# A two-block transformer on one core: the state space scan as a pipeline of eight blocks, its tables made earlier, and the experts' row tables made two experts ahead

## The chip, the cores and the metric

The kernel is one program on one core of a Trainium2 chip. The metric is the device time of one execution in microseconds (us), lower being better. The core has five engines with a queue each, and each queue runs in order: PE (matrix products), DVE (VectorE, elementwise), ACT (ScalarE, elementwise with functions), POOL (GpSimd, slow elementwise and indirect DMA), SP (SyncE, which here only issues DMAs). They meet at semaphores. [...] A planner places the instructions into the queues when the program is built: it walks through them by a priority, which is the order of the program with offsets, and by a simulated time line.

## The reference, cut to what matters

All of it is float32, batch 1, 512 tokens of width 1024. A first block (a retention and pooling mixer, 32 experts of which each token takes 4, a gated embedding layer called PLE) is followed by a second block with a state space layer, a feed-forward layer, a short convolution and another feed-forward layer. The two places that matter are these:

```python
# experts: gather the tokens of each expert, two products, scatter-add with the gate
flat_e = top_idx.reshape(-1); order = jnp.argsort(flat_e); tok = order // TOP_K
gu = lax.ragged_dot(xt[tok], w_gu, group_sizes) + b_gu[sorted_e]
...
# state space: 64 groups, 64 complex states each, 16 channels per group
abr = mag * jnp.cos(li * dt);  abi = mag * jnp.sin(li * dt)
...
_, _, xr, xi = lax.associative_scan(_ssm_combine, (a_r, a_i, bu_re, bu_im), axis=1)
y = einsum('ghp,blgp->blgh', c_re, xr) - einsum('ghp,blgp->blgh', c_im, xi) + d * h
y = jax.nn.gelu(y);  val, gate = jnp.split(y @ w_out, 2, -1);  return val * jax.nn.sigmoid(gate)
```

## The kernel before, in words

Large products are made in three passes each (high part by high part, high by low, low by high); `split` makes the two parts of a weight block with one ACT copy (L94) and one DVE subtraction (L95).

**Mixer** (`stage_mix`, about 0 to 245 us). Beside its own work it prepares the state space layer in the background: `S5Prepare.units` makes powers 0 to 8 of the complex state factor (`s_ar`, `s_ai`) and, on POOL and DVE, sixteen products `s_pp` (`power_product`, L1117 to L1121), which PE transposes. Background units are given out by `net.step`, with a priority 400 places later than where they stand. The mixer ends with the output product `w_out`, made in two halves. During the second half `Router` makes the norm of the hidden rows (`hnm`, POOL, L648), the logits, and the place of each token in its expert.

**Experts** (`Moe.experts`, about 286 to 1490 us). For expert e, `tables` turns the places into a table of the 88 rows to fetch (`tabim`: eight or more DVE comparisons L719, small PE products, DVE L725 to L727); one call makes it for two or four experts. `fetch` issues the indirect gather of these rows into `xg` (L744, POOL; two buffers), `prepare` transposes them on PE (`xt`, L758) and splits them. In the loop over e, `tables(e+1)` and `fetch(e+1)` stand at the head of turn e, `prepare(e+1)` behind `down(e-1)` in the middle of it. Weight blocks (`raw`, 1 MB) are loaded through nine buffers.

**State space layer** (`stage_s5`, about 1557 to 1771 us). The 512 tokens are 64 chunks of 8. For each of eight blocks k of 128 channels: `norm` (DVE, ACT), `to_chunks` (`zt`: 8 PE transposes, two copies), `to_groups` (`zu`: 8 transposes, a copy), `states` (`zs`: 32 products that give each chunk's own input to the state, a copy to `zX`). Then `scan` goes over the 63 chunk steps one by one, in two halves (blocks 0 to 4 and 5 to 7): a DVE product (L1518) and a DVE reduction (L1520) for each step and half. Then come `within` and `outputs` (`zy`, 16 products each, with the tables T and Q), `to_features` (`zf`, 32 products, GELU, split into `zgah` and `zgal`) and the product `ssm_out`. The table Q is made here: `readout` computes it on POOL (three operations of 128x512 for each of 16 parts) and sends it by SP to `q_d`, from where `load_q` takes it back.

## Time and profile before

| | us |
|---|---|
| three runs | 2694.55, 2701.68, 2705.07 |
| median | 2701.68 |
| profiled execution, its own time | 2704.24 |
| its span, first to last instruction | 2701.8 |
| PE busy in the span | 2558.8 (95%) |
| DVE busy | 1898.3 (70%) |
| ACT busy | 1374.8 (51%) |
| POOL busy | 430.1 (16%) |
| mean granted PE clock | 0.970 |

[...] "Busy" of an engine counts the time in which one of its instructions runs, waits inside an instruction included. PE's ends are modelled, so that consecutive products overlap a little in the list. The profiled execution's own time is 2.4 us more than its span, and 2.56 us more than the median.

### The profile page before, as it was taken

What the parts mean: (1) busy time and instruction counts of PE and PEld (TensorE: products, weight loads), DVE (VectorE), ACT (ScalarE), POOL (GpSimd) and SP (SyncE); (2) the same over time, 40 slices, a digit from 0 to 9 for tenths busy, and PEclk for the clock granted to TensorE, in tenths of its full rate; (3) what the DMA queues carried; (4) which work ended last, traced back from release to release, by engine and by line L of the source; (5) the groups of instructions that cost most, each with busy time, mean ns of one, the idle gap of its engine ahead of it and who ended that gap; (6) DMA issues with size and microseconds to landing.
All of it is one profiled execution on the core that took longest, in us unless ns stands there. A gap on an engine that the chain in (4) does not pass through costs nothing.

```text
span 2701.8 us, 31654 instructions
## 1 busy us (share of the span) xinstructions
PE 2558.8 (95%) x12270; PEld 1927.6 (71%) x12271; DVE 1898.3 (70%) x2410; ACT 1374.8 (51%) x1513; POOL 430.1 (16%) x252
## 2 busy tenths in 40 slices
PE   8999788999999999999999865999999999999998
PEld 6767555666666666666666755888788888888886
DVE  8974877999999999898988577775553544532333
ACT  7344565777777777777776644242122322322221
POOL 3362312031312112031200071000000000000000
PEclk9999898999999999999999987999999999999999
DMA  6435788999999999999996642754552222223221
GB/s 210 172 110 214 292 289 305 355 341 383 346 383 356 373 360 375 352 358 373 368 372 239 248 150 80 278 188 177 210 214 104 103 97 103 83 86 103 101 85 63
DMA packets 110432, 634.76 MB, mean 235 GB/s; under 512 B 16043, under 2 KB 21419, under 8 KB 43331
## 3 DMA queue, kind: packets, MB, share of 16 engines
q1 hardware_dynamic: 97971, 599.69, 59.6%
q0 software_dynamic: 11584, 28.27, 4.2%
q10 hardware_dynamic: 720, 4.72, 0.4%
q8 instruction: 98, 1.61, 0.2%
q14 instruction: 59, 0.48, 0.1%
HBM read 607.15 MB, written 28.61 MB: 235 GB/s over the span
## 4 chain that ended last, share of the span: by engine, by line
PE 66%; issue 18%; DMA 7%; DVE 6%; POOL 2%; ACT 2%; SPq 0%; POOLq 0%; DVEq 0%; ACTq 0%
PE gu L115 8%; PE gu L116 8%; PE gu L117 8%; PE mm L115 7%; PE mm L116 7%; PE mm L117 7%; PE dn L116 4%; PE dn L117 4%; PE dn L115 4%; DMA xg<-hn_d,tabim 2%; DMA acc_d<-y,tabim 2%; DMA raw<-in_w_ada 1%; PE mm L146 1%; DVE wl L95 1%; PE mm L147 1%
## 5 line engine op out<-in xcount | busy, mean ns | idle before, releaser
L95 DVE TENSOR_TENSOR el<-raw,eh 128x2048 fp32r<-128x2048 f32 (+1 forms) x396 | 874.5, 2221 | 99.3 <-ACT eh L94 93.2
L94 ACT ACTIVATE eh<-raw 128x2048 fp32r<-128x2048 f32 (+1 forms) x396 | 735.2, 1866 | 294.0 <-PE gu L117 209.9
L94 ACT ACTIVATE wh<-raw 128x1024 fp32r<-128x1024 f32 (+1 forms) x238 | 222.0, 981 | 478.2 <-PE mm L116 291.9
L116 PE MATMUL gu<-el,xh 128*88 128x512 f32 x1024 | 404.2, 395 | 0.0
L117 PE MATMUL gu<-eh,xl 128*88 128x512 f32 x1024 | 402.4, 393 | 0.0
L115 PE MATMUL gu<-eh,xh 128*88 128x512 f32 x1024 | 400.6, 397 | 0.0
L95 DVE TENSOR_TENSOR wl<-raw,wh 128x1024 fp32r<-128x1024 f32 (+1 forms) x238 | 265.5, 1148 | 79.9 <-ACT wh L94 79.6
L116 PE MATMUL mm<-nl,wh 128*128 128x512 f32 x816 | 318.3, 390 | 0.0
L115 PE MATMUL mm<-nh,wh 128*128 128x512 f32 x816 | 317.9, 390 | 0.0
L117 PE MATMUL mm<-nh,wl 128*128 128x512 f32 x816 | 316.8, 389 | 0.0
L117 PEld LDWEIGHTS gu<-eh,xl 128*88 128x88 f32 x1024 | 158.4, 155 | 78.4 <-issue 0.5
L116 PEld LDWEIGHTS gu<-el,xh 128*88 128x88 f32 x1024 | 158.9, 155 | 75.8 <-issue 0.5
L115 PEld LDWEIGHTS gu<-eh,xh 128*88 128x88 f32 x1024 | 158.3, 155 | 75.3 <-issue 0.3
L115 PE MATMUL dn<-eh,ath 128*88 128x512 f32 x512 | 204.0, 401 | 0.4
L116 PE MATMUL dn<-el,ath 128*88 128x512 f32 x512 | 202.5, 399 | 0.0
L117 PE MATMUL dn<-eh,atl 128*88 128x512 f32 x512 | 202.4, 396 | 0.0
L750 POOL DMA_INDIRECT acc_d<-y,tabim x32 | 93.8, 2931 | 633.0 <-ACT y L958 566.1
L744 POOL DMA_INDIRECT xg<-hn_d,tabim x32 | 142.2, 4444 | 318.9 <-PE xt L758 157.4
L115 PEld LDWEIGHTS mm<-nh,wh 128*128 128x128 f32 x816 | 153.2, 188 | 32.7
L117 PEld LDWEIGHTS mm<-nh,wl 128*128 128x128 f32 x816 | 153.2, 188 | 32.3
L116 PEld LDWEIGHTS mm<-nl,wh 128*128 128x128 f32 x816 | 153.2, 188 | 31.5
L1681 DVE TENSOR_TENSOR fs<-fs,mm 128x512 f32<-128x512 f32 x44 | 30.2, 687 | 205.8 <-PE mm L117 196.4
(468 smaller groups left out, 3925.7 us busy)
## 6 DMA issues: line engine op xcount, KB each, us to landing
raw<-in_w_gu SPq DMA_DIRECT2D x256, 1024.0 KB, 8.7
raw<-in_w_down SPq DMA_DIRECT2D x128, 1024.0 KB, 7.5
raw<-in_w_ada SPq DMA_DIRECT2D x45, 1024.0 KB, 4.9
raw<-in_w_ffn_in SPq DMA_DIRECT2D x44, 1024.0 KB, 4.8
raw<-in_w_ffn_out SPq DMA_DIRECT2D x32, 704.0 KB, 4.1
raw<-in_conv_in SPq DMA_DIRECT2D x12, 1024.0 KB, 4.9
raw<-in_ssm_out SPq DMA_DIRECT2D x8, 1024.0 KB, 5.0
raw<-in_w_out SPq DMA_DIRECT2D x4, 1024.0 KB, 4.8
```

The source lines that it names most:

```text
L94: nc.scalar.activation(h, x, AF.Copy)
L95: nc.vector.tensor_tensor(l, x, h.bitcast(F32), ALU.subtract)
L115: mm(ps, sh, mh, start=start, stop=False)
L116: mm(ps, sh, ml, start=False, stop=False)
L117: return mm(ps, sl, mh, start=False, stop=stop).ins
L146: self.nc.tensor.matmul(ps[c], wh, ah, start=k == 0, stop=False)
L147: self.nc.tensor.matmul(ps[c], wl, ah, start=False, stop=False)
L744: return net.nc.gpsimd.indirect_dma_start(out=dst, out_offset=None, in_=net.hn_d[:, :], in_offset=bass.IndirectOffsetOnAxis(ap=idx, axis=0 ...
L750: net.nc.gpsimd.indirect_dma_start(out=net.acc_d[:, :], out_offset=bass.IndirectOffsetOnAxis(ap=idx, axis=0), in_=src, in_offset=None, com ...
L1681: nc.vector.tensor_tensor(t, t, ps, ALU.mult)
```

## The change

Three things are changed, and some sizes with them.

The experts' row tables: turn e now makes `tables(e+2)`, in turn 0 too, while `fetch(e+1)` stays where it was. The number of weight blocks asked for ahead of the experts falls from 6 to 5 and from 9 to 8.

The scan: the state of a chunk step is turned back by its angle, so that its factor becomes real and `tensor_tensor_scan` runs over all chunks in one instruction. Each block k becomes a stage of a pipeline of its own: products with a cosine and sine table, an addition on POOL, the scan, products that turn it forward again, and four additions. The eight blocks run through `norm`, `to_chunks`, `to_groups`, `states`, `scan`, `outputs`, `to_features` with lags of 0 to 5.

The tables: `readout` moves to the end of the mixer, ahead of its output product, 11 of its 16 parts on POOL and 5 on DVE, and the cosine and sine tables are made beside it on DVE (`roots`, `turns`) and stored to `r_d`. The store to `e_d` and its loads go.

```diff
@@ stage_mix
         s5.rows(99)
+        net.bg = s5.tables(p2)
+        net.step(99)
@@ stage_mix_out
-        moe.prefetch(6)
+        moe.prefetch(5)
...
-        moe.prefetch(9)
+        moe.prefetch(8)
@@ Moe.experts
-            if e + 1 < NE:
-                if e:
-                    self.tables(e + 1)
-                    self.fetch(e + 1)
+            if e + 2 < NE:
+                self.tables(e + 2)
+            if e and e + 1 < NE:
+                self.fetch(e + 1)
@@ S5Prepare.tables (new)
+        u = pool.tile([128, 1280], F32, tag="w5", name="s_qu")
+        w = pool.tile([128, 1280], F32, tag="w5", name="s_turns")
...
+        def times(o, x, y, t):
+            for r, op in ((0, ALU.subtract), (1, ALU.add)):
+                vec.tensor_tensor(o[r], x[0], y[r], ALU.mult)
+                vec.tensor_tensor(t, x[1], y[1 - r], ALU.mult)
+                vec.tensor_tensor(o[r], o[r], t, op)
...
+        def roots():
...
+            for z in (lo, hi):
+                for n in (1, 2, 4):
+                    k = min(n, 7 - n)
+                    times(span(z, n + 1, n + k + 1), span(z, 1, k + 1), ...
+                if z is lo:
+                    times(span(hi, 1, 2), span(lo, 4, 5), span(lo, 4, 5), scratch[:, :H].unsqueeze(2))
+        def turns(b):
+            cs = self.pt.tile([128, 512], F32, tag="sb", name=f"s_tu{b}")
...
+            times([ov[:, r] for r in range(2)], ...
+            nc.sync.dma_start(net.r_d[:, b * 512:(b + 1) * 512], cs)
+        def readout(q, on_vector):
...
+            power_product(vec if on_vector else nc.gpsimd, t, ...
+            (nc.sync if on_vector else nc.gpsimd).dma_start(net.q_d[:, q * 512:(q + 1) * 512], t)
+        roots()
+        for q in range(G // GP):
+            readout(q, q % 3 == 2)
+            if q % 2:
+                turns(q // 2)
+            yield True
@@ stage_s5
+        def scan(k):
+            pv = sts.pop(k)
+            sh = [128, 4, 2, NCH]
...
+            nc.scalar.copy(ro[:, :, :, 1:], net.turn[:, 0, o]...to_broadcast([128, 4, 2, NCH - 1]))
+            def turned(x, sign):
+                w = [p2.tile(sh, F32, tag=f"zw{j}", ...) for j in range(2)]
+                tt(w[0], x, cos.unsqueeze(2).to_broadcast(sh), ALU.mult)
+                for r in range(2):
+                    if (r == 0) == (sign > 0):
+                        tt(w[1][:, :, r], x[:, :, 1 - r], sin, ALU.mult)
+                    else:
+                        nc.vector.scalar_tensor_tensor(w[1][:, :, r], x[:, :, 1 - r], -1.0, sin, ALU.mult, ALU.mult)
+                return w
+            w = turned(pv, 1)
+            nc.gpsimd.tensor_tensor(w[0], w[0], w[1], ALU.add)
+            x = p2.tile(sh, F32, tag="zx", name=f"zx{k}", bufs=2)
+            nc.vector.tensor_tensor_scan(x..., ro..., w[0]..., 0.0, ALU.mult, ALU.add)
+            w = turned(x, -1)
+            xq = XQ[k] = p2.tile([128, 2, 4, NCH], F32, tag="zxq", name=f"zxq{k}")
...
+            for h in range(2):
+                for r in range(2):
+                    i = slice(64 * h, 64 * h + 64)
+                    (nc.gpsimd if h == r else nc.vector).tensor_tensor(
+                        xq[64 * r:64 * r + 64, h, :, 1:], w[0][i, :, r, :NCH - 1], w[1][i, :, r, :NCH - 1], ALU.add)
...
+        for j in range(2):
+            nc.sync.dma_start(tv[:, 2048 * j:2048 * j + 2048], net.r_d[:, 2048 * j:2048 * j + 2048])
         load_t(0)
+        load_q(0)
         load_t(2)
-        with tc.high_priority(offset=-1000), tc.issue_after(net.rooted):
-            readout(net)
...
+        for n in range(NK + 6):
...
+            stage(norm, 0)
+            stage(to_chunks, 0)
+            stage(to_groups, 1)
+            stage(states, 2)
+            stage(scan, 2)
+            stage(outputs, 4)
+            if n in (5, 7):
+                load_q(n - 1)
+            stage(to_features, 5)
...
-        with tc.issue_after(net.scanned), tc.issue_after(net.kept):
-            net.linear_fm(a["ssm_out"], NK, lambda k: (gah[:, k], gal[:, k]), evac, rate=2)
+        net.linear_fm(a["ssm_out"], NK, lambda k: ga[k], evac, rate=2)
```

In `stage_s5` the copies of `to_chunks` all go to ACT, the high part of `to_features` to ACT and its low part to POOL, and the Q tables for blocks 0 to 3 sit in the two buffers `wh` of the weight splits, as the T tables of blocks 4 to 7 sit in `wl` before and after.

## Rows read from the trace of the kernel before

**Rows 1.** Page, busy time, share of the span and instructions.
```profile
PE 2558.8 (95%) x12270; PEld 1927.6 (71%) x12271; DVE 1898.3 (70%) x2410; ACT 1374.8 (51%) x1513; POOL 430.1 (16%) x252
```

**Rows 2.** Stretches of the state space layer: length, busy (count) by engine, clock, DMA.
```profile
1576.00:1600.00 24.00, 21.77 (x398) 20.14 (x398) 13.92 (x32) 20.05 (x34) 19.77 (x19) 1.00 0.35 123
1600.00:1650.00 50.00, 3.18 (x46) 2.96 (x44) 49.83 (x201) 16.36 (x42) 27.53 (x24) 0.56 0.26 95
1650.00:1678.00 28.00, 28.00 (x387) 26.87 (x387) 12.21 (x30) 17.55 (x31) 5.66 (x5) 0.93 0.37 130
```

**Rows 3.** Groups by line, DVE, 1560 to 1690 us: busy, mean ns, idle before.
```profile
L1518 DVE TENSOR_TENSOR zr<-a,zX 128x80 f32<-128x80 f32 (+1 forms) x124 | 47.7, 416 | 9.1 <-ACT zX L1497 8.3
L1520 DVE TENSOR_REDUCE zX<-zr 128x40 f32<-128x120 f32 (+1 forms) x124 | 26.5, 247 | 1.5 <-ACT zr L1516 0.5
```

**Rows 4.** PE in order of time: start, length, operation, count merged.
```profile
1574.40 1.20 PE L1493 MATMUL zs<-zU,s_pt 128*64 128x64 f32 x32
...
1578.32 1.09 PE L1472 MATMUL zt<-consts,zh 128*64 128x128 f32 x8
1579.34 0.71 PE L1480 MATMUL zu<-consts,zct 64*128 64x64 f32 x8
...
1594.44 8.46 PE L1562 MATMUL zy<-zT,zU 128*64 128x128 f32 x128
...
1662.48 2.65 PE L1573 MATMUL zy<-zQ,zxq 128*64 128x128 f32 x28
1665.06 1.90 PE L1583 MATMUL zf<-consts,zyt 64*64 64x64 f32 x32
...
1678.07 0.48 PE L146 MATMUL mm<-zgah,wh 128*128 128x512 f32 x1
```

**Rows 5.** DVE groups by form, 1560 to 1690 us, columns as in rows 3.
```profile
L1592 DVE TENSOR_TENSOR zgal<-zg,zgah 128x512 fp32r<-128x512 f32 x4 | 2.7, 683 | 0.0
```

**Rows 6.** DVE in order of time, two steps of the scan.
```profile
1586.36 0.24 DVE L1518 TENSOR_TENSOR zr<-a,zX 128x80 f32<-128x80 f32 x1
...
1591.13 1.02 DVE L1518 TENSOR_TENSOR zr<-a,zX 128x80 f32<-128x80 f32 x1
```

**Rows 7.** POOL groups by form, 1560 to 1640 us.
```profile
L1121 POOL TENSOR_TENSOR ro<-ro 128x512 f32<-128x512 f32 x16 | 20.4, 1275 | 0.7
```

**Rows 8.** Two stretches of the experts, columns as in rows 2.
```profile
330.00:350.00 20.00, 7.43 (x32) 5.01 (x31) 9.51 (x9) 4.76 (x4) 10.49 (x2) 0.66 0.75 270
425.00:443.00 18.00, 5.60 (x26) 4.11 (x25) 7.15 (x6) 5.15 (x7) 8.25 (x4) 0.62 0.78 264
```

**Rows 9.** Chain that ended last, 325 to 440 us: start, length, what.
```profile
328.23 18.16 DMA xg<-hn_d,tabim
346.53 1.41 PE xt L758 x8
...
415.91 22.99 DMA xg<-hn_d,tabim
```

**Rows 10.** Two stretches around the mixer's output product, columns as in rows 2.
```profile
200.00:246.00 46.00, 44.41 (x207) 37.09 (x206) 16.74 (x32) 17.24 (x46) 4.95 (x7) 0.89 0.68 257
246.00:286.00 40.00, 26.57 (x166) 23.33 (x165) 29.32 (x92) 22.14 (x41) 15.16 (x13) 0.78 0.31 106
```

**Rows 11.** POOL groups by form, 85 to 200 us.
```profile
L1121 POOL TENSOR_TENSOR s_pp<-s_pp,s_tp 128x512 f32<-128x512 f32 x12 | 18.5, 1555 | 0.1
...
L1117 POOL TENSOR_TENSOR s_pp<-s_ar,s_bc 128x512 f32<-128x512 f32 x12 | 16.1, 1348 | 6.0 <-PE sw L1262 4.2 <-DVE s_ar L1174 1.8
```

**Rows 12.** DVE groups by form, 85 to 200 us.
```profile
L1174 DVE TENSOR_TENSOR s_ar<-s_ar,s_la 128x256 f32<-128x256 f32 x1 | 0.4, 421 | 0.0
```

**Rows 13.** POOL in order of time, router and first gather.
```profile
246.25 2.40 POOL L648 TENSOR_TENSOR hnm<-h,gb 128x1024 f32<-128x1024 f32 x1 [30.57 <-DVE h L525]
...
279.42 1.34 POOL L744 DMA_INDIRECT xg<-hn_d,tabim  x1 [8.59 <-DVE el L95]
280.78 2.22 POOL L542 DMA_DIRECT2D acc_d<-h  x4
```

More of the change, by code (lines that the diff above doesn't have):

```diff
@@ L814, in prefetch @@
             src = net.a[nm][e][b]
-            q = j % (9 + EXTRA)
-            if q < 6:
-                t = net.load(src, self.raw2, "raw2")
-            else:
-                t = net.load(src) if q < 9 else net.load(src, self.raw3, "raw3")
+            q = j % 9
+            t = net.load(src, self.raw2, "raw2") if q < 6 else net.load(src)
             self.loaded.append(t)
@@ L1172, in units @@
             sincos(net, ang, ei, lam, t[:, :256], t[:, 256:])
+            if b:
+                for h in range(2):
+                    r = slice(64 * h, 64 * h + 64)
+                    for j, v in enumerate((ar[r, 8, h::2], lam[r, 3 * G + h::2], ai[r, 8, h::2])):
+                        nc.vector.tensor_copy(net.turn[r, j], v)
             tt(ei, er, ei, ALU.mult)
@@ L1350, in stage_ple @@
         net.pt = []
-        for z in range(2):
-            t = net.op.tile([128, 32, 128], F32, tag="op", name=f"s_pt{z}")
-            for q in range(2):
-                o = slice((2 * z + q) * 2048, (2 * z + q + 1) * 2048)
-                with tc.issue_after(copied[-1]):
-                    nc.scalar.dma_start(t[:, 16 * q:16 * q + 16].rearrange("p g x -> p (g x)"), net.p_d[:, o])
+        for z in range(4):
+            t = net.op.tile([128, 16, 128], F32, tag="op", name=f"s_pt{z}")
+            with tc.issue_after(copied[-1]):
+                nc.scalar.dma_start(t.rearrange("p g x -> p (g x)"), net.p_d[:, z * 2048:(z + 1) * 2048])
             net.pt.append(t)
@@ L1529, in stage_s5 @@
-        T = {}
+                        nc.tensor.matmul(pv[64 * h:64 * h + 64, mm, r],
+                                         net.pt[k // 2][:, 8 * (k % 2) + e, 64 * r:64 * r + 64],
+                                         U[k][:, e], start=True, stop=True)
+        def scan(k):
+            pv = sts.pop(k)
+            sh = [128, 4, 2, NCH]
+            o = slice(4 * k, 4 * k + 4)
+            cos, sin = tab[:, o, 0], tab[:, o, 1]
+            ro = rho[k % 2]
+            nc.scalar.copy(ro[:, :, :, 1:], net.turn[:, 0, o].unsqueeze(2).unsqueeze(3).to_broadcast([128, 4, 2, NCH - 1]))
+            def turned(x, sign):
+                w = [p2.tile(sh, F32, tag=f"zw{j}", name=f"zw{k}_{sign}_{j}") for j in range(2)]
+                tt(w[0], x, cos.unsqueeze(2).to_broadcast(sh), ALU.mult)
[8 more added lines that the diff above has]
+            x = p2.tile(sh, F32, tag="zx", name=f"zx{k}", bufs=2)
+            flat = "p m r c -> p (m r c)"
+            nc.vector.tensor_tensor_scan(x.rearrange(flat), ro.rearrange(flat), w[0].rearrange(flat), 0.0, ALU.mult, ALU.add)
+            w = turned(x, -1)
+            xq = XQ[k] = p2.tile([128, 2, 4, NCH], F32, tag="zxq", name=f"zxq{k}")
+            nc.gpsimd.memset(xq[:, :, :, 0], 0.0)
+            for h in range(2):
+                for r in range(2):
+                    i = slice(64 * h, 64 * h + 64)
+                    (nc.gpsimd if h == r else nc.vector).tensor_tensor(
+                        xq[64 * r:64 * r + 64, h, :, 1:], w[0][i, :, r, :NCH - 1], w[1][i, :, r, :NCH - 1], ALU.add)
@@ L1587, in to_features @@
                                  AF.Gelu_apprx_tanh)
-            if k < 4:
-                nc.scalar.activation(gah[:, k], t, AF.Copy)
-            else:
-                nc.vector.tensor_copy(gah[:, k], t)
-            (nc.gpsimd if k < 4 else nc.vector).tensor_tensor(gal[:, k], t, gah[:, k].bitcast(F32), ALU.subtract)
+            if k % 2 == 0:
+                g = op.tile([128, 2, 2, S], F32R, tag="op", name=f"zga{k}")
+                ga[k], ga[k + 1] = [(g[:, 0, j], g[:, 1, j]) for j in range(2)]
@@ L1594, in stage_s5 @@
+            h, l = ga[k]
+            nc.scalar.activation(h, t, AF.Copy)
+            nc.gpsimd.tensor_tensor(l, t, h.bitcast(F32), ALU.subtract)
+        for j in range(2):
+            nc.sync.dma_start(tv[:, 2048 * j:2048 * j + 2048], net.r_d[:, 2048 * j:2048 * j + 2048])
         load_t(0)
+        load_q(0)
         load_t(2)
-        with tc.high_priority(offset=-1000), tc.issue_after(net.rooted):
-            readout(net)
-        for k in range(NK):
-            norm(k)
-        scans = []
@@ L1601, in stage_s5 @@
-        LEAD = 20
-        for z in range(2):
-            ks = range(ZK[z], ZK[z + 1])
-            for n in range(len(ks) + 2):
-                if n < len(ks):
-                    to_chunks(ks[n])
-                if 0 <= n - 1 < len(ks):
-                    to_groups(ks[n - 1])
-                if 0 <= n - 2 < len(ks):
-                    states(ks[n - 2])
-            scans.append(scan(z))
-            for _ in range(LEAD if z == 0 else 0):
-                next(scans[0])
-        for _ in range(NCH):
-            for x in scans:
-                next(x, None)
@@ L1617, in stage_s5, with stage @@
-        for x in scans:
-            list(x)
-        gah = op.tile([128, NK, S], F32R, tag="op", name="zgah")
-        gal = op.tile([128, NK, S], F32R, tag="op", name="zgal")
+        load_q(2)
         load_t(4)
         load_t(6)
-        for k in range(NK):
-            within(k)
-        for k in range(0, NK, 2):
-            load_q(k)
-        for k in range(NK + 1):
-            if k < NK:
-                outputs(k)
-            if k:
-                to_features(k - 1)
+        for n in range(NK + 6):
+            def stage(f, lag):
+                if 0 <= n - lag < NK:
+                    f(n - lag)
+            stage(norm, 0)
[7 more added lines that the diff above has]
+            stage(to_features, 5)
```

156 lines of the change are left out of this document (62 added, 94 removed).

## Prediction

> **What bounds the kernel now.** I read the page's busy shares first, then windows over the whole span for the places where PE stands, then in each such place the list of waits, the chain and the engines in order of time. PE is busy 95% of the span [rows 1], so time is won only where PE has nothing to do or runs at its low clock. Three places matter. In the state space layer PE works 3.18 of 50 us between 1600 and 1650 while DVE is at 49.83; the granted clock there averages 0.56 [rows 2]. That is the scan: 124 products of 0.416 us and 124 reductions of 0.247 us, 51.6 and 30.6 us by these means, spread over two halves that take turns [rows 3]. In the experts PE is without work for 20.00 - 7.43 = 12.6 us around 340 and 18.00 - 5.60 = 12.4 us around 434 [rows 8]; in both the chain shows an indirect gather of `xg`, issued at 328.23 and 415.91 and landing 18.2 and 23.0 us later [rows 9], behind the row table that turn e makes for expert e+1. The windows of the other turns show PE filled. The third place, 246 to 286 us, is the router: PE works 26.57 of 40 us [rows 10]; the change removes nothing there, but puts work in front of it.
>
> **Scan and pipeline.** What stands between the first block's states (issued at 1574.40, done at 1575.6) and the first product of `ssm_out` (1678.07) is 102.5 us [rows 4]. Of the new pipeline I cost one block on each engine.
>
> PE keeps all its products: 1.09 + 0.71 + 1.20 for `zt`, `zu`, `zs`; 8.46/8 = 1.06 for the first half of `zy`; 2.65/28 x 16 = 1.51 for the second; 1.90 for `zf`. That is 7.5 us a block [rows 4]. (The second half takes 95 ns a product against 66 in the first; its states now lie contiguous, and at 66 ns the block would be 7.0.)
>
> DVE loses the 82 us of steps and gains, per block, `norm`, three products out of PSUM, the scan, three products out of SBUF and two half-height additions. Of 128x512 a product takes 0.68 [rows 5], of half that width 0.42 [rows 12]. With `norm` at 0.7: 0.7 + (0.68 + 2 x 0.42) x 2 + 2 x 0.42 = 4.6 us, plus the scan instruction, which no row shows. Below, it is a product of its size, 0.68 [rows 5]; above, it saves nothing against today's steps: product and reduction together are 0.663 us for 64 columns on average, eight times that is 5.3 [rows 3]. I take 0.68, since its operands are those of the product. [...]
>
> DVE also waits for POOL. A step's 80-column product takes 0.24 us, and 1.02 where POOL streams its 128x512 products; the reductions beside it do not stretch [rows 6]. So an operation with two SBUF inputs can lose up to 0.78. Six of the new DVE operations are such ones (scan, three products, two additions). POOL's new work per block is two operations of 1.28 [rows 7] and two half additions of at most half that, 3.8 us, about half of a block's time; I take half of 0.78 for each, 2.4 us. DVE then needs 4.6 + 0.68 + 2.4 = 7.7 us a block, PE 7.5. ACT loses the copies to `zX` and of the kept states and gains one copy for the factors; it was at 20.05 of 24 us while it fed three stages [rows 2], and stays below PE. I take 7.8 us a block. After the last scan come half a `zy` (1.06), a copy of about 0.6, `zf` (1.90) and hand-overs, together 4 us. So 1575.6 + 8 x 7.8 + 4.0 = 1642.0, and **the stage gives back 1678.1 - 1642.0 = 36 us**. Bounds: PE at 7.0 and all else hidden, 1635.6, 42 us; DVE with a scan of 5.3 and six full waits, 4.6 + 5.3 + 4.7 = 14.6 us a block, 1696.4, a loss of 18.
>
> What moves with it: POOL's `readout` (16 x 3 operations) and its 16 stores on SP leave the stage; nothing waits for `q_d` there any more. SP gets two loads of the cosine table at the head of the stage, behind which the 32 loads of T and the first loads of Q queue; the table is wanted at the first scan, T and Q at the first `zy`, some 15 us later. I cost them at nothing; if the first load is late, it shifts the whole pipeline by its lateness. The weights of `ssm_out` no longer wait for the scan, but for the `wh` and `wl` buffers in which Q and T sit; these fall free after blocks 1, 3, 5 and 7, the first pair two blocks ahead of its use. Zero; without that cover it is one split, some 2 us.
>
> **Row tables.** `tables(2)` is made in turn 0 and `tables(4)` in turn 2, so when turn e begins, `fetch(e+1)` has its rows and waits only for its buffer, which `prepare(e-1)` has left a turn before. A gather that starts a dozen us before 328 lands in time even at 18.2 us; the second has a whole turn. The work is the same, only earlier; the same operations cost the same. The two holes close: 12.6 + 12.4 = 25.0. After each hole PE restarts at the low level: the granted clock averages 0.66 and 0.62 in the two windows [rows 8], so in the first it is at 1.0 for 0.32 x 20 = 6.4 us, all before the hole ends at 346.53 [rows 9], which leaves at least 3.5 us of work at half speed, 1.7 lost; the same again at the second. **28.4 us.** Between nothing (the gathers stay late) and this I take this. The added wait: a table's buffer is one of three, so the table of expert 4 now waits for the scatter of expert 0, with DVE's splits queued behind; there is half a turn for it, and I cost it at nothing. `prefetch` gives one block less ahead of the start; that block is the sixth, wanted several blocks after PE begins. Zero, and one load if not.
>
> **Tables in the mixer.** POOL gains 33 products of 1.35 to 1.56 us in that company [rows 11], 48 us, and 11 DMA issues of 2.22/4 = 0.56 [rows 13], 6: 54 us. DVE gains 15 operations of 0.68 (10), 48 of 256 columns at 0.42 [rows 12] (20) and 48 small ones of the roots at about 0.24 [rows 6] (12): 42 us. They can start when the last score tiles fall free, about 200. Until 246 POOL has 46 - 5.0 = 41 us free and DVE 46 - 16.7 = 29 [rows 10]: both lack 13 us. At 246.25 POOL's queue comes to `hnm` [rows 13], and behind it are the router's chain, the first gather at 279.42 and so PE. From 246 to 286 POOL has 25 us free and DVE 10.7. Queued behind these on SP are the new stores (13) and, after them, the first weight loads and the stores of `hn_d`. The cost lies between 0 (the rest runs in those gaps) and 13 + 44 x 0.78 = 47 us (each of the 44 POOL operations also holds a DVE one up, and all of it stands ahead of the router). I take **10 us lost**: the shortage of 13, less a part for the gaps.
>
> **Sum.** 2704.24 - 36 - 28.4 + 10 = 2649.8 for an execution like the profiled one. That one lay 2.56 us above the median of the runs shown, so 2647 for the median.
>
> **Rivals.**
> The mixer's tables hold the router up for the whole 47 us: 2647 + 37 = 2684. For it: DVE has just 29 us free there, and the waits of [rows 6] come on top. Against it: POOL's products ran beside a busy DVE before, lengthened by only a quarter [rows 7, 11].
> The gathers stay late, because POOL's queue or the planner puts them behind a scatter: the holes remain, 2647 + 28 = 2675. For it: a gather issued at 328.23 needed 18.2 us [rows 9]. Against it: its table was the last thing to be ready.
> DVE takes 14.6 us a block (a scan that saves nothing, full waits): the stage loses 18 instead of gaining 36, 2647 + 54 = 2701.
> [...]
> **Slower:** the in-order queues let no block overlap the next, because DVE's turned products of block k stand ahead of `norm` of block k+1 and wait for POOL and the scan. One block is then a chain: 0.7 + 0.7 + 1.1 + 1.2 + 0.7 + 0.6 + 1.2 + 1.5 + 1.3 + 0.7 + 1.5 + 0.7 + 1.5 + 0.6 + 1.9 = 15.9 us, with some 15 hand-overs of about 0.2 about 19; eight blocks are 152 us from 1568, 1720. The stage loses 42: 2647 + 78 = 2725. It decides from about 14 us a block upwards. Against it: the lags in the new loop are there to let stages alternate in each queue.
>
> **Chances.** Forecast 0.66, its own range 2628 to 2668; mixer 0.12; gathers 0.10; DVE-bound 0.04; low clock 0.03; chained blocks 0.05. A measurement of this kernel can tell about 0.5% from no change, 13.5 us, so faster is below 2688. The mixer's rival lies so near that limit that a quarter of it counts as no change: faster 0.66 + 0.09 + 0.10 = 0.85, same 0.03 + 0.04 + 0.03 = 0.10, slower 0.05. The range reaches up to the mixer's 2684, which takes in the late gathers and most of the forecast, and down to a free mixer (-10), a PE-bound pipeline (-6) and the spread of the runs (-7): 2624. What is left out above and below is about 0.2.
>
> **What will show it.** In the state space layer: DVE below 90%, no window with PE under half, `ssm_out` starting some 66 us after the first states, the scan instruction's own length, and the two-input products at 0.7 to 1.1. In the experts: no wait of `xt` for `xg` above 2 us after the first, gathers for experts 2 and 4 issued before 316 and 400, clock 1.00 throughout. Around the router: `hnm` not much later than 250, and the first `xt` within 10 us of where it was (286). I am wrong if the first `xt` comes after 310, if the clock in the pipeline stays at 0.5, or if a block takes more than 10 us.

## The result and the profile after

The changed kernel takes 2717.82 us (median of 5 runs, 2715.99 to 2722.53). The kernel before, on the same chip, takes 2694.71 (5 runs, 2694.35 to 2705.07). The ratio is 1.0079, with an interval from 1.0063 to 1.0096: the change makes the kernel 0.8% slower. The forecast was 2647. The profiled execution took 2717.82 us, its span 2715.8.

Where the time went is read from the starts of the first PE instruction on one tile of each stage, and from the last product of the last feed-forward stage (us; the kernels right of "after" are the experiments further down):

| from, to | before | after | pad | rows | moved | dve16 | aligned |
|---|---|---|---|---|---|---|---|
| start, first `xt` of the experts | 285.9 | 328.8 | 328.8 | 282.4 | 315.4 | 292.6 | 290.5 |
| first `xt`, first `ht` of the per-layer stage | 1216.3 | 1203.2 | 1200.3 | 1208.6 | 1201.4 | 1203.1 | 1202.9 |
| first `ht`, first `zt` | 66.3 | 65.8 | 67.2 | 69.2 | 68.5 | 67.5 | 68.0 |
| first `zt`, first product of `ssm_out` | 109.5 | 75.0 | 75.3 | 109.7 | 77.3 | 77.4 | 77.3 |
| `ssm_out`, first `nh` | 97.4 | 100.2 | 98.0 | 97.4 | 100.2 | 100.3 | 100.2 |
| first `nh`, last `fh` | 912.3 | 929.3 | 912.8 | 908.8 | 912.7 | 907.9 | 906.3 |

So after against before is +42.9 ahead of the experts, -13.1 in them, -0.5, -34.5 in the state space stage, +2.8, and +17.0 in the last stages, which the diff doesn't touch: +14.4 for the last product (the rounded terms add up to 14.6), +14.0 for the span. The medians differ by 23.1 us. The profiled execution of before was a long one, 2704.24 against a median of 2694.71, so about 9 us of the loss can't be placed in these stages. Some may lie ahead of the experts, whose start is known to about 5 us only: `skew` (below), with the instructions of the kernel before, has its first `xt` at 281.5 instead of 285.9. PE is busier than before, and the kernel is slower:

```profile
PE 2600.7 (96%) x12270; PEld 1937.8 (71%) x12271; DVE 1935.9 (71%) x2331; ACT 1340.6 (49%) x1465; POOL 413.2 (15%) x280
```

The state space stage of after, columns as in [rows 2]. DVE no longer fills it, PE does, at a granted clock of 0.98 of full speed; in the tail the clock is 0.63:

```profile
1600.00:1650.00 50.00, 49.22 (x742) 44.70 (x741) 40.84 (x62) 33.09 (x55) 26.25 (x30) 0.98 0.30 97
1650.00:1675.00 25.00, 18.93 (x156) 16.89 (x155) 17.59 (x24) 7.44 (x11) 8.65 (x8) 0.63 0.25 85
```

A block's `zy` on PE at clock 1.00 (1631 to 1636 us), 96 and 99 ns a product in the two halves, where [rows 4] has 66 for the first:

```profile
1631.60 1.53 PE L1597 MATMUL zy<-zT,zU 128*64 128x128 f32 x16
...
1633.66 1.58 PE L1602 MATMUL zy<-zQ,zxq 128*64 128x128 f32 x16
```

Its DVE groups, 1600 to 1660 us (busy, mean ns, idle before), where [rows 3] had the 124 steps. The scan instruction itself takes 1.22 us:

```profile
L1558 DVE TENSOR_TENSOR_SCAN zx<-zrho,zw 128x512 f32<-128x512 f32 x8 | 9.8, 1221 | 5.5 <-POOL zw L1555 5.4
L1546 DVE TENSOR_TENSOR zw<-zs,ztab 128x512 f32<-128x512 f32 x8 | 5.4, 681 | 0.9 <-PE zs L1531 0.9
...
L1551 DVE SCALAR_TENSOR_TENSOR zw<-zs,ztab 128x256 f32<-128x256 f32 x8 | 3.3, 410 | 0.0
...
L1565 DVE TENSOR_TENSOR zxq<-zw_-1_0_14283,zw_-1_1_14284 64x252 f32<-64x252 f32 x2 | 1.8, 898 | 0.1
```

The tail on PE (start, length, operation, idle before and releaser). The second half of `zy` takes 2.85 us and `zf` 3.3, where it was 1.58 above and 1.90 in [rows 4]:

```profile
1657.75 2.85 PE L1602 MATMUL zy<-zQ,zxq 128*64 128x128 f32 x16 [3.39 <-POOL zga L1624]
1661.27 3.31 PE L1614 MATMUL zf<-consts,zyt 64*64 64x64 f32 x32 [0.68 <-ACT zyt L1605]
1665.24 2.86 PE L1602 MATMUL zy<-zQ,zxq 128*64 128x128 f32 x16 [0.66 <-DVE zxq L1565]
1668.77 3.30 PE L1614 MATMUL zf<-consts,zyt 64*64 64x64 f32 x32 [0.67 <-ACT zyt L1605]
```

The windows in which [rows 8] has the two holes, in after: PE is full. As the experts begin 43 us later here, the same work comes later too, but the only wait of PE for `xg` in after is the one before its first `xt`.

```profile
330.00:350.00 20.00, 20.00 (x99) 13.54 (x98) 13.57 (x27) 11.91 (x11) 1.14 (x1) 0.86 0.55 209
425.00:443.00 18.00, 18.00 (x82) 12.06 (x81) 16.36 (x10) 12.76 (x9) 6.04 (x2) 1.00 1.02 332
```

The mixer's output product and the router, which [rows 10] shows before. DVE (third number after the length) goes from 16.74 to 44.27 of 46 us and then stands at 39.52 of 40. PE does 29.94 us of work in the first window instead of 44.41 and makes up for a part in the second (32.77 instead of 26.57); in the third it has 17.00, where before, in the last line, has 43.32 and is among the experts already:

```profile
200.00:246.00 46.00, 29.94 (x133) 25.35 (x134) 44.27 (x86) 14.93 (x43) 29.33 (x29) 0.74 0.33 124
246.00:286.00 40.00, 32.77 (x142) 26.07 (x140) 39.52 (x62) 8.61 (x13) 28.14 (x25) 0.87 0.43 155
286.00:330.00 44.00, 17.00 (x103) 14.67 (x101) 31.13 (x98) 16.18 (x32) 15.65 (x15) 0.60 0.90 333
```
```profile
286.00:330.00 44.00, 43.32 (x208) 29.30 (x209) 37.26 (x68) 27.94 (x22) 9.40 (x7) 0.93 0.90 346
```

On POOL, what [rows 13] shows at 246.25 and 279.42 now comes at 273.00 (the last `hnm` at 307.55) and 315.84:

```profile
273.00 2.50 POOL L648 TENSOR_TENSOR hnm<-h,gb 128x1024 f32<-128x1024 f32 x1 [4.47 <-DVE h L525]
...
307.55 2.40 POOL L648 TENSOR_TENSOR hnm<-h,gb 128x1024 f32<-128x1024 f32 x1 [8.63 <-DMA hn_d<-hnm]
315.84 4.33 POOL L744 DMA_INDIRECT xg<-hn_d,tabim  x1 [5.89 <-DVE el L93]
```

And the stages that nobody touched. One group of PE from 1800 to 2680 us, first of before, then of after: the same products, 390 and 395 ns long. From 2000 to 2200 us before has 886 of them and after 868 at the same clock 1.00, one in 225.7 and in 230.4 ns:

```profile
L115 PE MATMUL mm<-nh,wh 128*128 128x512 f32 x796 | 310.1, 390 | 0.0
```
```profile
L113 PE MATMUL mm<-nh,wh 128*128 128x512 f32 x793 | 313.0, 395 | 0.0
```

### The profile page after: what moved, and what is told of

Same layout as the page of the kernel before. It is cut to its first block, busy times and chain, and to the rows that moved or that the text cites. A ratio compares the mean times of both kernels' runs of the same rounds, so it can differ in the third digit from the quotient of the medians.

```text
span 2715.8 us, 31609 instructions
## 1 busy us (share of the span) xinstructions
PE 2600.7 (96%) x12270; PEld 1937.8 (71%) x12271; DVE 1935.9 (71%) x2331; ACT 1340.6 (49%) x1465; POOL 413.2 (15%) x280
## 4 chain that ended last, share of the span: by engine, by line
PE 65%; issue 19%; DVE 12%; DMA 3%; ACT 1%; POOL 1%; SPq 0%; another core or an unknown queue 0%; POOLq 0%; DVEq 0%; ACTq 0%
PE gu L114 8%; PE gu L115 7%; PE gu L113 7%; PE mm L113 7%; PE mm L115 7%; PE mm L114 7%; PE dn L114 4%; PE dn L115 4%; PE dn L113 4%; DVE el L93 2%; PE mm L144 1%; DVE wl L93 1%; PE mm L145 1%; DMA acc_d<-y,tabim 1%; PE mm L142 1%
## 5 line engine op out<-in xcount | busy, mean ns | idle before, releaser
L92 ACT ACTIVATE eh<-raw 128x2048 fp32r<-128x2048 f32 (+1 forms) x396 | 717.7, 1858 | 77.8 <-PE gu L115 58.0
L744 POOL DMA_INDIRECT xg<-hn_d,tabim x32 | 124.6, 3895 | 554.8 <-PE at L758 270.1
L1071 DVE SCALAR_TENSOR_TENSOR adaj<-raw,adac 128x1024 bf16<-128x1024 f32 x90 | 111.5, 1239 | 63.9 <-DMA raw<-in_w_ada 63.1
```

Of the source, the lines that this page charges most:

```text
L92: nc.scalar.activation(h, x, AF.Copy)
L744: return net.nc.gpsimd.indirect_dma_start(out=dst, out_offset=None, in_=net.hn_d[:, :], in_offset=bass.IndirectOffsetOnAxis(ap=idx, axis=0 ...
L1071: nc.vector.scalar_tensor_tensor(junk, ws[q], 1.0, c, ALU.mult, ALU.mult, accum_out=m[:, o:o + 1])
```

## The experiments

Three things had to be told apart: why untouched stages are slower, what in the mixer costs 42.9 us, and why closing 25 us of holes, forecast to be worth 28, gives 13. Below, "pitch" is the mean distance between the starts of neighbouring 512-column products in the trace, those under 200 and over 300 ns left out.

**Placement: `pad`, `skew`, `padall`.** The diff replaces `a8` (512 bytes a partition) with `turn` (384), so every tile behind it lies 128 bytes lower.

`pad`:

```
-        net.turn = net.rt.tile([128, 3, G // 2], F32, name="turn")
+        net.turn = net.rt.tile([128, 4, G // 2], F32, name="turn")
```

> The changed kernel with one edit: the tile `turn` is 32 floats (128 bytes a partition) wider, so that everything placed behind it lies where it lay in the kernel before. The instructions and their order are those of the changed kernel. Placement theory: the 14 to 17 us by which the feed-forward and convolution stages are slower come from the addresses of the operands; the 512-column products start every 226.7 ns there again instead of 232.4 (389 instead of 393 to 395 ns long), the stretch from the first product of the first feed-forward stage to the last of the second goes from 928.7 back to about 912 us, and the time falls from 2717.8 to about 2701, a little less if the experts gain too. Rival, the chip or the run: the pitch stays at 232 ns and the time at 2718 within 3 us.

Measured: 2695.69 us, ratio to before 0.9991 (0.9981 to 1.0002); against after's 2717.8, 22 us. The last stages take 912.8 us, their pitch is 226.7 ns again, and the group is back at 390 ns:

```profile
L113 PE MATMUL mm<-nh,wh 128*128 128x512 f32 x788 | 307.0, 390 | 0.0
```

The first `xt` stays at 328.8. So 128 bytes of padding are worth 0.8%, and without the shift the change is neither faster nor slower.

`skew` (in the kernel before):

```
-        stage_ffn(net, 0)
-        stage_conv(net)
-        stage_ffn(net, 1)
+        for n, stage in ((96, lambda: stage_ffn(net, 0)), (32, lambda: stage_conv(net)), (16, lambda: stage_ffn(net, 1))):
+            with tc.tile_pool(name=f"skew{n}", bufs=1) as skew:
+                skew.tile([128, n], F32, name=f"skew{n}")
+                stage()
```

> The kernel before with one edit: an unused tile ahead of each of the three last stages, 384 bytes a partition wide for the first feed-forward stage, 128 for the convolution, 64 for the second feed-forward stage. The instructions are those of the kernel before. Placement theory, with the pitch set by the address modulo 512: the first feed-forward stage comes to lie at 192, as in the changed kernel, and runs at 232.4 ns a product instead of 226.7; the second comes to lie at 384, where the convolution lay before, and runs at 228.9; the convolution at 0, which no run has shown, at anything from 226 to 234. First stage about 9 us longer, second about 3.5, in sum 12 us slower (between 10 and 18). Rival, the chip or the run: no stage moves by more than 1 us and the time is that of the kernel before.

Measured: 2710.14 us, ratio 1.0049 (1.0035 to 1.0063), 12.6 slower than the 2697.54 of before beside it. The pitches are 232.38, 233.33 and 228.89 ns. The window of the first stage has after's count, that of the last one lies between:

```profile
2000.00:2200.00 200.00, 199.21 (x868) 161.31 (x867) 90.88 (x125) 56.05 (x77) 1.03 (x1) 1.00 0.32 112
...
2400.00:2600.00 200.00, 200.00 (x876) 164.10 (x875) 64.22 (x74) 49.84 (x65) 0.00 (x0) 1.00 0.28 96
```

`padall` (in the changed kernel; this pool lies ahead of the weights' buffers too):

```
-        self.half = c.tile([128, 1], F32, name="half")
+        self.half = c.tile([128, 33], F32, name="half")[:, :1]
```

> The changed kernel with 128 bytes a partition of padding ahead of everything, so that the weights' buffers move together with the operands behind `turn`. If the pitch depends on where the moving operand lies relative to the weights (modulo 512), nothing changes: 232.4 ns in the feed-forward stages, 2718 us. If it depends on the operand's own address, the feed-forward stages run at 226.7 ns as in `pad` and the time is about 2696 us.

Measured: 2717.04 us, ratio 1.0067 (1.0046 to 1.0088); 862 products from 2400 to 2600 us, pitch 232.4 in the second feed-forward stage and 233.0 in the first. So here the operand's own address did not count: with operand and weights both moved by 128 bytes the pitch stayed at the 232.4 of the changed kernel, with the operand alone moved (`pad`) it was 226.7.

**Row tables: `rows`, `rows2`.** In the kernel before:

```
-            if e + 1 < NE:
-                if e:
-                    self.tables(e + 1)
-                    self.fetch(e + 1)
+            if e + 2 < NE:
+                self.tables(e + 2)
+            if e and e + 1 < NE:
+                self.fetch(e + 1)
```

> The kernel before with the row tables alone changed: turn e makes the table for expert e+2, the gathers stay where they were. Holes theory: the two stands of PE in front of `xt` near 340 and 434 us close, 25 to 28 us, and nothing else moves: 2695 - 27 = about 2668. Rival: the table that is made earlier puts its DVE work in front of the splits, and every fourth expert waits for `el` twice, 2.0 us in each period of four experts, as the changed kernel shows: 25 - 14 = 11 us gained, about 2684. Rival: the gathers stay late, nothing is gained.

Measured: 2688.31 us, ratio 0.9964 (0.9951 to 0.9976), 9.2 us; the experts take 1208.6 instead of 1216.3. The second hole is closed. Of the first, 12.6 us, 8.1 are left: the gather is issued at 318.21, ten us earlier than in [rows 9], and still takes 17.4 us to land, while PE, whose first `xt` is at 282.4, comes for the rows at 327.7. And nine waits for `el` have come (the gather in the chain that ended last; PE's waits, 287 to 500 us, then 500 to 1480):

```profile
318.21 17.43 DMA xg<-hn_d,tabim
```
```profile
PE xt L758 <- DMA xg<-hn_d,tabim: 9.3, 2, 8.1
```
```profile
PE gu L116 <- DVE el L95: 7.7, 9, 1.4
```

`rows2` makes only the tables of experts 2 and 4 early:

```
-            if e + 1 < NE:
-                if e:
+            if e in (0, 2):
+                self.tables(e + 2)
+            if e and e + 1 < NE:
+                if e > 3:
                     self.tables(e + 1)
-                    self.fetch(e + 1)
+                self.fetch(e + 1)
```

> The kernel before with the row tables of experts 2 and 4 alone made earlier (in turns 0 and 2); those of experts 8, 12 and so on are made in the turn before, as in the kernel before. If the two waits for `el` in every period of four experts come from making each table a turn earlier, the holes close and the period stays what it was: the experts take 1188 to 1192 us (1216.3 before, 1208.6 in `rows`) and the time falls by 23 to 28 us to about 2672. Rival: the waits come from closing the holes (the loads of weights have less lead once PE no longer stands), then the experts take about 1208 us as in `rows` and the gain is about 9.

Measured: 2696.58 us, ratio 0.9999 (0.9985 to 1.0013); the experts take 1212.0. Both holes are closed here (1.7 us are left of the first). Of the waits of `gu` for `el` 1.1 us are left, and others stand in their place: from 500 us on PE waits for `xg` three times, which it doesn't do in the kernel before. The rival that the waits come with the closing of the holes is nearer, though in another shape than it said.

```profile
PE xt L758 <- DMA xg<-hn_d,tabim: 15.4, 3, 7.7
```

What `rows` has lost shows in what ACT waits for, 500 to 1480 us, first before, then `rows`. Before, it waits 168 us for PE to leave a buffer: the splits are as far ahead as the buffers let them. In `rows` that is 12 us, and ACT waits for products that are just being made. In `rows2` it is 104.1: there most of the lead is still found, and PE stands for `xg` all the same.

```profile
ACT eh L94 <- PE gu L117: 168.0, 171, 3.9
...
ACT sg L771 <- PE gu L939: 7.3, 6, 1.7
```
```profile
ACT sg L771 <- PE gu L939: 127.6, 50, 5.4
...
ACT eh L94 <- PE gu L117: 12.0, 13, 3.9
```

**The mixer: `moved`, `dve16`, `alldve`, `idle`, `best`.** `moved` is `pad` with `roots` and `turns` (pieces of a quarter) on POOL beside the experts:

```
-        roots()
         for q in range(G // GP):
             readout(q, q % 3 == 2)
-            if q % 2:
-                turns(q // 2)
             yield True
...
+            if e >= 4:
+                with tc.issue_after(self.fetched), tc.high_priority(offset=-net.low):
+                    next(turning, None)
```

> The changed kernel, with the wider `turn`, and the cosine tables moved: `roots` and `turns` leave the mixer's output product and DVE, and are made by POOL beside the experts 4 to 31, in 32 pieces; the 16 readouts stay in the mixer. Shortage theory: in the changed kernel DVE spends 54 us of 200 to 300 us on `roots` and `turns` and stands at 10 of 10, and that is what holds the router up: without them the first `xt` of the experts comes at 286 to 300 us instead of 328.8, and the time falls by about 29 to 43 us against the kernel with the wider tile. Rival, POOL's readouts and their stores hold the router up: the first `xt` stays beyond 315 us. The experts lose something, since POOL's products now run beside their splits: 0 to 20 us, read from the time of four experts (145.3 us in the kernel before).

Measured: 2687.30 us, ratio 0.9959 (0.9946 to 0.9972), 8.4 below `pad`. The first `xt` comes at 315.4, just beyond the bound that was set for the rival: taking 54 us of work from DVE gives back only 13.4 of the 42.9. The trace shows why, here DVE and then POOL in order of time. A DVE operation of 8 columns takes 4.33 us, while POOL runs three readout operations, and one of 4 columns in the router's own chain takes 5.01 (a mean of 0.22 in `dve16`):

```profile
220.29 1.67 DVE L1120 TENSOR_TENSOR s_qu<-s_ai,s_c 128x512 f32<-128x512 f32 x1
221.88 1.08 DVE L460 TENSOR_TENSOR grs<-grs,consts 128x8 f32<-128x8 f32 x1
222.99 4.33 DVE L461 TENSOR_TENSOR gmean<-gmean,grs 128x8 f32<-128x8 f32 x1
...
266.46 5.01 DVE L690 TENSOR_SCALAR ex<-ex,sm 128x4 f32<-128x4 f32 x1
```
```profile
223.51 1.12 POOL L1120 TENSOR_TENSOR s_qu<-s_ai,s_c 128x512 f32<-128x512 f32 x1
224.59 1.11 POOL L1118 TENSOR_TENSOR s_q<-s_ar,s_c 128x512 f32<-128x512 f32 x1
...
226.01 1.28 POOL L1122 TENSOR_TENSOR s_q<-s_q,s_qu 128x512 f32<-128x512 f32 x1
```

`dve16` is `moved` with no readout on POOL:

```
-            readout(q, q % 3 == 2)
+            readout(q, True)
```

> The kernel `moved` (cosine tables beside the experts) with one edit: all 16 readouts on DVE instead of 5, none on POOL. In `moved` the first `xt` came at 315.4 us, 29.5 later than in the kernel before. Theory that POOL's streaming does it (small DVE operations of the router stretched to 1 to 2.5 us, `hnm` queued behind readouts on POOL): with POOL free of them DVE's 48 products keep about 0.68 us, 33 us in all, which fits into the 40 us that DVE had free between 200 and 286: first `xt` at 282 to 300 us, time about 15 to 30 us below `moved`. Rival, the mere amount of work ahead of the router: DVE now has 21 us more than in `moved`, and the first `xt` comes at 315 us or later.

Measured: 2667.09 us, ratio 0.9903 (0.9877 to 0.9929), first `xt` at 292.6. DVE has 33 products more than in `moved` and the first `xt` is 22.8 us earlier. From 195 us to the first `xt`, DVE's operations in `moved` are 28 us longer in sum than by the median of the same line and shape in `dve16`. Not all of the delay arises beside the readouts: at the last `hnm` `moved` is 14.4 us behind (284.4 and 270.0), at the first gather 27.1 (304.24 and 277.10). In between, when POOL's readouts are over, one of the last stores of `hn_d` takes 10.8 us to land (2.6 in `dve16`), and 16 pieces of `el` stand ahead of the gather in DVE's queue (none there in `dve16`). What the stores and the order in DVE's queue cost by themselves was not tried. The same operation of 8 columns, and the products around it:

```profile
214.42 0.16 DVE L461 TENSOR_TENSOR gmean<-gmean,grs 128x8 f32<-128x8 f32 x1
214.50 0.68 DVE L1118 TENSOR_TENSOR s_q<-s_ar,s_c 128x512 f32<-128x512 f32 x1
215.10 0.69 DVE L1120 TENSOR_TENSOR s_qu<-s_ai,s_c 128x512 f32<-128x512 f32 x1
```

`alldve` is the same edit in `pad`: everything in the mixer, all of it on DVE.

> The changed kernel, with the wider `turn`, and one edit: all 16 readouts on DVE, none on POOL; roots, cosine tables and readouts all stay in the mixer's output product, on DVE. Streaming theory: with POOL quiet DVE's work is 48 x 0.69 + 48 x 0.42 + 12 = 65 us, 25 more than the 40 that it had free between 200 and 286: first `xt` at about 286 + 25 = 311 us (305 to 317), 12 to 24 earlier than in the changed kernel (328.8) although DVE has 33 more products; time 2675 to 2684. Rival, the amount of work alone: DVE had 66 us of tables in the changed kernel and has 87 now, and the first `xt` comes at 345 us or later.

Measured: 2676.86 us, ratio 0.9924 (0.9904 to 0.9944), first `xt` at 299.3, 12 earlier than I expected and 29.5 earlier than in the changed kernel, with more work on DVE. The groups of `turns` from 195 us on, after and then `alldve`, show what an operation costs beside POOL and without it. From 195 us to the first `xt`, DVE's operations in after are 35 us longer in sum than by their medians in `alldve`, against a delay of 29.5:

```profile
L1275 DVE TENSOR_TENSOR s_tu<-s_tu,s_turns 128x256 f32<-128x256 f32 x16 | 14.3, 893 | 0.3
L1274 DVE TENSOR_TENSOR s_turns<-s_turns 128x256 f32<-128x256 f32 x16 | 10.4, 653 | 0.1
```
```profile
L1275 DVE TENSOR_TENSOR s_tu<-s_tu,s_turns 128x256 f32<-128x256 f32 x16 | 10.2, 638 | 0.0
...
L1274 DVE TENSOR_TENSOR s_turns<-s_turns 128x256 f32<-128x256 f32 x16 | 6.6, 411 | 0.0
```

`idle` takes the readouts out of the mixer too, onto POOL beside the experts in halves:

```
-        net.bg = s5.tables(p2)
-        net.step(99)
...
+            t = w[:, g // 2 % 2 * 256:g // 2 % 2 * 256 + 256]
+            power_product(pool, t, u, er, ei, y1, y2, ALU.subtract)
+            pool.dma_start(net.q_d[:, g * 128:g * 128 + 256], t)
```

> The changed kernel, with the wider `turn`, and both kinds of tables out of the mixer: POOL makes the cosine tables and then the readouts beside the experts 4 to 25, in pieces of half the size; the powers go through memory as in the kernel before. If the tables alone held the router up, the first `xt` is back at 281 to 287 us, the state space stage keeps its 75 us, and the time is 2695.7 - 43 = 2653 us plus what POOL's products cost the experts (1.2 us for the cosine tables in `moved`; 0 to 8 expected in all). Rival: something else in the changed mixer (the shorter prefetch, the order of the queues) has a part, and the first `xt` stays beyond 295 us.

Measured: 2695.15 us, ratio 0.9997 (0.9984 to 1.0011). The first `xt` is at 281.6, so the tables were all that held the router up (`best`, with the same mixer, has 275.6). But the experts take 1251.9 us, 49 more than in `dve16`; 0 to 8 was wrong. POOL's products, 1.27 us for twice the width in [rows 7], are lengthened beside DVE's splits (the group from 500 to 1480 us), the splits themselves hardly (2.33 us against 2.30 in `dve16`), and PE stands 24 times for `el` (its waits, 290 to 1535):

```profile
L1119 POOL TENSOR_TENSOR s_turns<-s_turns 128x256 f32<-128x256 f32 x32 | 84.0, 2626 | 1.4
```
```profile
PE gu L114 <- DVE el L93: 23.5, 24, 2.3
PE gu L113 <- ACT eh L92: 8.8, 2, 6.8
PE xt L756 <- DMA xg<-hn_d,tabim: 8.6, 2, 7.9
```

The three kinds are 40.9 us. `dve16` has 9.9 of the first and, behind its first `xt`, none of the others; the third is what is left of the first hole, as in `rows`, where POOL makes no tables. So 22 of the 49 us are waits for splits and 9 are for the gather. The rest was not followed up.

`best` is `idle` with the row tables of `rows2`.

> The kernel `idle` with the row tables as in `rows2`. If the three gains add (holes, state space stage, a mixer as before): `idle` less a further 15 to 17 us, about 2640 us, faster than both kernels. If the waits for `el` come from closing the holes, the same as `idle`.

Measured: 2699.28 us, ratio 1.0007 (0.9992 to 1.0022), the experts 1254.9 us. That is 51.8 us more than in `dve16`, and the three gains don't add up.

**Two more: `aligned`, `ohm`.** `aligned` is `dve16` with three unused tiles of 16, 112 and 40 floats ahead of the mixer's operands, ahead of the convolution and beside the per-layer product:

```
+            skew = eh.enter_context(tc.tile_pool(name="skew2", bufs=1))
+            skew.tile([128, 16], F32, name="skew2")
             act = eh.enter_context(tc.tile_pool(name="mact", bufs=8, reuse_waits="tile"))
```

> The kernel `dve16` with unused tiles that bring the operands of three stages to the weights' place modulo 512: 64 bytes ahead of the mixer's operands, 160 beside those of the per-layer product, 448 ahead of the convolution. If equal places give 226.7 ns everywhere, the convolution's 768 products go from 228.9 to 226.7 ns (1.7 us), the per-layer product's 192 from 234.3 to 226.7 (1.5 us) and the mixer's first products from 233.3 and 228.9 to 226.7 (up to 2 us): 3 to 5 us below `dve16`. If the equal place is a coincidence of the feed-forward stage, these pitches stay as they are or go elsewhere.

Measured: the pitch of the convolution is 226.67 instead of 228.89, of the per-layer product 226.9 instead of 234.3, of the mixer's first products 226.7 and 227.8 instead of 229.0 and 233.5, as forecast. The convolution's group, 2200 to 2320 us, is 389 ns long (392 and 394 before). The time is 2665.94 us, ratio 0.9888 (0.9869 to 0.9906), the best of all; the step from `dve16` (1.2 us in the medians) is too small to be told from none by the times, only by the pitches.

```profile
L113 PE MATMUL mm<-ch,wh 128*128 128x512 f32 x48 | 18.7, 389 | 0.0
L114 PE MATMUL mm<-cl,wh 128*128 128x512 f32 x48 | 18.7, 389 | 0.0
```

`ohm` is `aligned` with the comparisons of the late row tables on POOL:

```
-            nc.vector.tensor_scalar(oh, net.iota_s, posm(e, i), None, op0=ALU.is_equal)
+            eng = nc.gpsimd if n == 4 and name != "m4" else nc.vector
+            eng.tensor_scalar(oh, net.iota_s, posm(e, i), None, op0=ALU.is_equal)
```

> The kernel `aligned` with one edit: the 16 comparisons that begin each row table of four experts (from expert 8 on) run on POOL instead of DVE. In `aligned`, as in every kernel with the early row tables, a period of four experts takes 147.8 to 148.9 us, two products in it wait about 1.1 us each for `el`, and DVE spends 16 x 0.26 = 4.2 us and some waiting on these comparisons just ahead. If DVE's extra work at that point, with no lead over PE left, is what lengthens the period, the waits go and the period is 145 to 147 us: 10 to 14 us over the phase, time about 2653. Rival: PE's pace is set elsewhere, the period stays at 148 to 149 and the time at 2666.

Measured: 2672.72 us, ratio 0.9919 (0.9899 to 0.9939), 6.8 more than `aligned` in the median; four experts take 149.4 to 151.0 us. The waits of `gu` for `el` shrink from 9.9 to 3.6 us, but a comparison of 0.26 us on DVE is one of 1.51 on POOL, and PE waits for it (POOL's group and PE's wait, 500 to 1480 us). It decides nothing: the cure brought its own wait.

```profile
L720 POOL TENSOR_SCALAR ohm<-iota_s,posm 128x88 bf16<-128x88 f32 x85 | 127.4, 1514 | 16.8 <-PE sl L722 16.8
```
```profile
PE sl L722 <- POOL ohm L720: 10.2, 11, 1.7
```

## Why the prediction was wrong

**State space stage: right, by misses that cancel.** 36 us forecast, 34.5 measured. The products of the scan out of PSUM and SBUF cost what the rows said (0.68 and 0.41), the half-height additions beside POOL 0.9 instead of 0.42, the scan 1.22 instead of the 0.68 that I took. By the trace it takes 1221 ns against 681 of a product of its size, 1.8 times as long: that its operands are those of the product did not give it the product's length. The scan's length cost nothing that shows, since PE was full (49.22 of 50 us from 1600 to 1650). PE's block is neither my 7.5 us nor the 7.0 of the lower bound, but 1.09 + 0.71 + 1.20 + 1.53 + 1.58 + 1.90 = 8.0: the second half of `zy` did not fall to 66 ns a product, and the first rose to 96. The first product of a block on DVE comes at 1605.1 in block 0 and at 1654.5 in block 7, 7.06 us apart. That this is near 7.0 is luck: the second half of `zy` and the `zf` of the last two blocks still stand behind 1654.5. They make the tail: the first states end at 1605.0, and from 1605.0 + 8 x 7.06 to 1672.8 it is 11.3 us where I had 4. There PE waits for POOL, DVE and ACT between the last blocks (3.39, 0.66 and 0.68 us), its clock is 0.50 from 1657 to 1673 us, and these `zy` and `zf` take nearly twice as long (2.85 against 1.58 us, 3.30 against 1.90).

**Mixer: the step that failed.** I took 10 us "lost: the shortage of 13, less a part for the gaps"; it is 42.9. The shortage was reckoned with DVE's 42 us at quiet lengths. I knew from [rows 6] that a product of 0.24 takes 1.02 beside POOL, used that for the state space stage, and here only for the upper bound. What I set against the rival, that POOL's products were lengthened by only a quarter [rows 7, 11], looks at the wrong engine: it is DVE's many short operations that are stretched, the router's own among them. `alldve` splits the 42.9: 13.4 are left when the same work is all on DVE, so 29.5 go with the 11 readouts on POOL, shown by one edit. That they act by stretching DVE's operations is shown by the lengths, 35 us more in sum; the edit also moves 11 stores to SP and changes the order in DVE's queue, and the part of these was not separated. My rival "held up for the whole 47" had the mechanism and nearly the price, and I gave it 0.12.

**Row tables: right in what closes in the changed kernel, wrong in what it is worth.** There both holes closed and the gathers were in time. 28.4 us forecast, 13.1 measured, and 7.7 alone in `rows`. The step that failed is to count the holes at their full length because "the same operations cost the same": I had not asked what is late next. PE now waits 7.7 us for `el`, twice in four experts, and 2.9 us are lost to placement (`pad` takes 1200.3); some 5 of the missing 15.3 us stay without an account. In `rows`, where the experts begin 46 us earlier than in the changed kernel, the gather of the first hole starts ten us earlier than in before, not the dozen that I reckoned with, and PE comes for its rows at 327.7 already, 6 us earlier than in before: the 8.1 us left of the first hole and the 7.7 for `el` are 15.8 of the 20.7 us that are missing there. Why `el` is late is argued, not shown: while PE stood, DVE and ACT ran ahead, and this lead paid for later waits. That the lead is gone in `rows` is shown by what ACT waits for; but `rows2` keeps most of it and waits for `xg`, `ohm` replaced one wait by another, and none brought the pace back. This stays open.

**Placement: not in the sum at all.** 17.0 us in the last stages, 22 in the whole kernel, from a tile that became 128 bytes shorter. `pad`, `skew` and `padall` show it.

Put together, for an execution like the profiled one: 2649.8 + 32.9 (mixer) + 15.3 (row tables) + 17.0 (placement) + 1.5 (state space stage) + 2.8 - 0.5 (`ssm_out`, per-layer) = 2718.8, against 2717.8. As a change between medians the forecast (2701.68 to 2647) is off by 77.8 us, about 9 more than this sum has, since the median of before is 2694.71 in the runs beside the changed kernel. Of the signs that I had named, the first `xt` after 310 was the one that came true.

The edits at which I put nothing (the loads of the cosine table, one block less of prefetch, the added wait of the third table) cost nothing that could be seen: `idle`, with the short prefetch, has its first `xt` at 281.6.

## What to carry to other kernels

Moving work from a busy engine to an idle one was no gain here, where DVE's operations were 35 us longer in sum beside POOL: price each operation of both, the short ones of the critical chain above all, at its length beside the other, and try everything on one engine (here 33 products more on DVE made the kernel 20 us faster). A stall need not be worth its length (25 us of holes gave 13.1 and 7.7 here): ask what is late next, and which engines run ahead during the stall. And when the size of any tile changes, look whether products in untouched stages have changed their length; if they have, pad before judging the rest (128 bytes a partition were worth 22 us here).

## What the runs showed of the hardware

The first thing is the pitch of back-to-back products of 512 columns, as the traces of this case's runs have it in the stages below (both operands float32r, 128 rows and columns; clock 1.00 from 2000 to 2600 us). It differed with the distance in bytes of the streamed operand from the weights in their partition, given less whole multiples of 512. The distances are reckoned from the tiles' places in the program, which no profile shows; the steps between the rows of one stage are those of the edits:

| streamed operand minus weights | pitch, ns | where |
|---|---|---|
| 0 | 226.7 | feed-forward of before and `pad`, convolution of `aligned` and `ohm` |
| 32 | 233.6 | per-layer product of `padall` |
| 64 | 228.9 | convolution of before, second feed-forward of `skew` |
| 96 | 233.3 | `ssm_out` of after |
| 160 | 234.3 | per-layer product of all but `aligned`, `ohm` and `padall` |
| 192 | 233.3 | convolution of `skew` |
| 224 | 233.3 | `ssm_out` of before and `pad` |
| 384 | 232.4 | feed-forward of after, first of `skew` |
| 448 | 233.3 | convolution of after |

Whether 512 is the true period was not tried; 256 would fit these rows as well (192 and 448 have the same pitch), 128 would not (0 and 384).

The second thing is how long DVE's short operations were beside POOL's. The operation of 8 columns took 0.16 us in `dve16`, which has no readout on POOL, and 4.33 in `moved`, from 222.99 to 227.32, while POOL ran three readout operations (223.51 to 227.29); one of 4 columns took 0.21 in the kernel before and 5.01 in `moved`. The 128x512 readouts on DVE, with two SBUF inputs, took 0.69 in `dve16` and up to 1.67 in `moved`; copies of 128x512 out of PSUM (0.68 and 0.68) and reductions of 128x128 (0.38 and 0.37) kept their lengths. But the one of 4 columns has one SBUF input and a factor for each partition, and the cast of `tri`, with a single input, took 1.12 in `moved` instead of 0.22, so two inputs, as I had it in the prediction, are not needed here. POOL's operations were longer too: 2.63 us for 256 columns in `idle`, beside splits of 2.33 on DVE, against 1.27 for 512 in [rows 7]. What holds either engine's operation, no trace shows.
